# A decoder layer on one core: the places of matmul operands in memory, and a running product without an extra column

## The chip, the cores and the metric

The kernel runs on one core of a Trainium2 chip, in one launch. The core has TensorE (PE, the matmuls; its weight loads are listed apart as PEld), VectorE (DVE), ScalarE (ACT), GpSimd (POOL) and SyncE (SP), which here only issues transfers. Each has its own queue, in the order in which the program was written, and they meet at semaphores. The metric is device time in microseconds, the median of several runs. Lower is better.

## The reference

One decoder layer in float32: 1024 tokens of width 1024, and a final norm.

```python
h = rmsnorm(x, w_norm_mix)
proj = h @ w_mix_in                       # 1024 x 3592
y_sc = sc_b * causal_dwconv(sc_c * sc_h, w_sconv)
# gated delta rule in chunks of 64, 4 heads of 128, after a convolution and silu of q, k, v
y_gdn = rmsnorm(gated_delta_rule(q, k, v, g, beta), w_gdn_norm) * silu(z)
# stick-breaking attention, 4 heads of 64: for keys s < query t
#   A[t,s] = sigmoid(z_ts) * prod over s<j<t of (1 - sigmoid(z_tj));  y_sb = A @ v
x = x + concat([y_sc, y_gdn, y_sb]) @ w_mix_out
h = rmsnorm(x, w_norm_ffn)
gate, val = split(causal_dwconv(h @ w_ffn_up, w_ffn_conv))   # 2 x 2816 columns
x = x + (silu(gate) * val) @ w_ffn_down
return rmsnorm(x, w_norm_final)
```

## The kernel before

Every wide product is made of three fp32r matmuls: each operand is split into a rounded part h and a rest l, and h h, h l and l h are added up. A matmul has 128x128 weights and 512 moving columns. The program has four stages with such matmuls.

The input projection (lines 298 to 304, `mm_cm`) makes 26 column tiles of the projection. The moving operands are the activations xh and xl, four buffers each of the tag x8; the weights are tiles of the tags wh and wl, split from a loaded tile of the tag wr. The output projection (lines 1275 to 1296) has the output weights `wo` as moving operand (x8 again, after xh and xl are done) and the layer's outputs yh (tag s2) and yl (tag cv) as weights: 8 blocks of 48 matmuls, with transposes between. The up projection (line 1516, `product`) computes 22 pairs of column tiles with seven block products each, in the manner of Strassen; a product is 12 matmuls in a row. Its moving operands are the factors fB11, fB21, fB22, fT1 (tag e8) and fT2, fT3, fT4 (tag x8), and its weights come from `op_tile` (line 1449), which takes tiles of s2, wh, wl and wr in turn. The down projection (line 1682, `dn_mm`) has seven products of 11 slices, 12 matmuls each; `dn_tiles` (line 1640) takes both operands of a slice from the same list of tags, and its tiles' names end in the tag (P67wr, P67wh).

A tag is a set of equal buffers in SBUF, made by `T` (line 192) from one pool, in the order of their first use and with the size of the largest tile of the tag, rounded up to 32 bytes for each partition. In the built kernel, a tag's buffers so begin at these byte addresses modulo 256: x8 at 224; e8, cv and at at 32; wr, wh and wl, of 4224 bytes, at 32 and 160 in turn; the nine buffers of s2, of 2080 bytes (520 columns, line 204), each 32 further than the one before. A product's slices within a tile lie 512 or 2048 bytes apart.

From the input projection to the output projection the order of work on all engines is made by a planner, the class `Flow` (line 74): the parts of the layer are generators that yield requests (engine, estimated time, rank), wait for named events, and take and give counted buffers; the planner plays them against each other and records the instructions in the order in which it grants them. The wide matmuls of the projection are what PE gets between the pieces of attention, and then of the recurrence. From the up projection on, the order is written out by hand.

The attention works on pieces of 128 queries and up to 512 keys (`sb_piece`, line 606). ACT makes two sigmoids, om = 1 - sigmoid and sg = sigmoid; DVE runs a product from the last key to the first over om (line 641); POOL multiplies sg by om one column to the right (line 647), for which om has one more column: 1 for a query block's last piece (a memset, line 633) or else the carry out of the piece before (a copy, line 639). PE then transposes sg. In the recurrence, `prep2` (line 899) builds the inverse of a triangular block for every chunk of 128 tokens out of inverses of 32x32 blocks, in small matmuls (pw, py), after `inverse` (line 858) has run on DVE; `chain` (line 1095) then takes the chunks one after another.

Of the kernel before, what the change touches and what calls it, by code (L numbers as in the profile page):

```python
# [9 lines left out]
F32 = mybir.dt.float32  # L10
# [6 lines left out]
P = 128  # L17
# [4 lines left out]
GH = 4  # L22
# [162 lines left out]
def trunk(ctx: ExitStack, tc: tile.TileContext, xT, x, cst, wcm, wsv, wout, wnf, wup, wdn, wfin, out):  # L185
    nc = tc.nc
    sb = ctx.enter_context(tc.tile_pool(name="sb", bufs=1))
    dr = ctx.enter_context(tc.tile_pool(name="dr", bufs=1, space=DRAM))

    BUFS = dict(x8=8, e8=8, at=2, cv=4, s2=9, wr=2, wh=2, wl=2)  # L190

    def T(shape, dt, tag, name, bufs=None):
        return sb.tile(shape, dt, tag=tag, name=name, bufs=bufs or BUFS.get(tag, 1))

    def x8(shape, name, dt=F32):
        return T(shape, dt, "x8", name)

    def e8(shape, name, dt=F32):
        return T(shape, dt, "e8", name)
# [1 line left out]
    def cv(name, dt=F32, tag="cv"):  # L201
        return T([P, 1024], dt, tag, name)

    def s2(name, dt=F32, shape=(P, 520)):
        return T(list(shape), dt, "s2", name)

    def small(shape, name, bufs=1):
# [2 lines left out]
    def f32(ap):  # L210
        return ap.bitcast(F32)

    def copy(out_, in_, scale=None):
        if scale is None:
            nc.scalar.activation(out_, in_, AF.Copy)  # L215
        else:
            nc.scalar.activation(out_, in_, AF.Copy, scale=scale)  # L217

    def tt(eng, out_, a, b, op):
        eng.tensor_tensor(out_, a, b, op=op)  # L220
# [4 lines left out]
    mul, add, sub = ALU.mult, ALU.add, ALU.subtract  # L225
# [39 lines left out]
    def ms(name):  # L265
        return pp.tile([P, 512], F32, tag="ms", name=name, bufs=4)
# [53 lines left out]
    rb = T([P, L], F32, "rb", "rb")  # L320
# [17 lines left out]
    for ks in ((0,), (1,), (2, 3), (4, 5), (6, 7)):  # L338
        n = len(ks) * P
# [30 lines left out]
    fl = Flow(mm=2, ms=4, cv=1, s2=9, wr=2, wh=2, wl=2, at=2, e8=6, x8=0)  # L370

    def pe(ns, due=None):
        return "PE", ns, due, None

    def act(n, table=None, cls=None):
        return "ACT", T_ACT[0] + T_ACT[1] * n, cls, table

    def dve(n, port=True, per=T_DVE, cls=None):
        return "DVE", per[0] + per[1] * n, cls, port

    def pool(n, cls=None):
        return "POOL", T_POOL[0] + T_POOL[1] * n, cls, None

    def sp(kb, cls=None):
        return "SP", 2000 + 5 * kb, cls, None

    def take(tag, n=1):
        return "take", tag, n

    def wait(*what):  # L390
        return "wait", what

    def now(*what):
        fl.happen(what)
# [24 lines left out]
    def halves(r):  # L419
        return slice(64 * r, 64 * r + 64), slice(64 - 64 * r, 128 - 64 * r)  # L420
# [175 lines left out]
    for h in range(SH):  # L596
        for tb in range(NB):
            hi = (tb + 1) * P
            while hi > 0:
                lo = max(0, hi - 512)  # L600
                PIECES.append((h, tb, lo, hi))
                hi = lo
# [3 lines left out]
    def sb_piece(i, due):  # L606
        h, tb, lo, hi = PIECES[i]
        j, r = h // 2, h % 2
        own, _ = halves(r)
        n, w, nb = (tb + 1) * P, hi - lo, (hi - lo) // P  # L610
        nm = f"{h}_{tb}_{lo}"
        t = slice(tb * P, (tb + 1) * P)
        if i >= SB_AHEAD:
            yield wait("piece", i - SB_AHEAD)
        yield wait("sq", j, r)
        yield wait("sk", j, r)
        yield take("s2", 2)
        yield take("ms")
        yield pe(2 * max(60, w * 0.448) + (60 if hi == n else 0), due)
        pz = ms("pz" + nm)  # L620
        nc.tensor.matmul(pz[:, 0:w], lhsT=qa[j][:, r, t], rhs=kk_[j][:, r, lo:hi], start=True, stop=False)
        nc.tensor.matmul(pz[:, 0:w], lhsT=ql[j][:, r, t], rhs=kk_[j][:, r, lo:hi], start=False, stop=hi < n)
        if hi == n:
            nc.tensor.matmul(pz[:, w - P:w], lhsT=identr, rhs=causal, start=False, stop=True)
        yield act(w, "sig")
        sg, om = s2("sg" + nm), s2("om" + nm)
        nc.scalar.activation(om[:, 0:w], pz[:, 0:w], AF.Sigmoid, scale=-0.125)  # L627
        yield act(w, "sig")
        nc.scalar.activation(sg[:, 0:w], pz[:, 0:w], AF.Sigmoid, scale=0.125)
        fl.give("ms")  # L630
        if hi == n:
            yield pool(0)
            nc.gpsimd.memset(om[:, w:w + 1], 1.0)
            init = 1.0
        else:
            yield wait("scan", i - 1)
            yield pool(8)
            init = oms.pop(i - 1)[:, 0:1]
            nc.gpsimd.tensor_copy(om[:, w:w + 1], init)
        yield dve(w, per=T_SCAN)  # L640
        nc.vector.tensor_tensor_scan(om[:, 0:w][:, ::-1], om[:, 0:w][:, ::-1], om[:, 0:w][:, ::-1], init, op0=mul, op1=ALU.bypass)  # L641
        if hi < n:
            fl.give("s2")
        oms[i] = om
        now("scan", i)
        yield pool(w)
        tt(nc.gpsimd, sg[:, 0:w], sg[:, 0:w], om[:, 1:w + 1], mul)
        if lo == 0:
            fl.give("s2")
        yield take("ms")  # L650
        yield pe(109 * nb, due)
        pa = ms("pa" + nm)
        for b in range(nb):
            nc.tensor.transpose(out=pa[:, b * P:(b + 1) * P], in_=sg[:, b * P:(b + 1) * P], identity=ident)  # L654
        fl.give("s2")
        yield take("at")
        yield act(w)
        at = T([P, 4, 2, P], F32R, "at", "at" + nm)
        pav = pa[:, 0:w].rearrange("p (b t) -> p b t", b=nb)
        copy(at[:, 0:nb, 0, :], pav)  # L660
        yield dve(w, False)
        tt(nc.vector, at[:, 0:nb, 1, :], pav, f32(at[:, 0:nb, 0, :]), sub)
        fl.give("ms")
        if i > 0:
            yield wait("po", i - 1)
        for b in range(lo // P, hi // P):
            if i < 4:
                yield wait("v", b)
        if hi == n and tb % 2 == 0:
            yield take("ms")  # L670
            pos[h, tb // 2] = ms(f"po{h}_{tb}")
        po = pos[h, tb // 2]
        yield pe(118 * nb, due)
        for b in range(nb):
            s = lo // P + b
            nc.tensor.matmul(po[:, (tb % 2) * 256:(tb % 2) * 256 + 256], lhsT=vst[s // 4][:, s % 4, h * P:(h + 1) * P],
                             rhs=at[:, b, :, :].rearrange("p a t -> p (a t)"),
                             start=hi == n and b == 0, stop=lo == 0 and b == nb - 1)
        fl.give("at")
        now("po", i)  # L680
        now("piece", i)
        if i % PER == PER - 1:
            now("sb", j)
            fl.give("e8", 3 + 2 * j)
        if lo == 0 and tb % 2 == 1:
            pv = po.rearrange("p (a two t) -> p a two t", a=2, two=2)
            yield take("s2")
            yield act(256)
            yb = s2(f"yb{h}_{tb}")
            d = yb[:, 0:256].rearrange("p (a t) -> p a t", a=2)  # L690
            copy(d, pv[:, :, 1, :])
            yield dve(256, False)
            tt(nc.vector, d, pv[:, :, 0, :], d, add)
            fl.give("ms")
            yield dve(256)
            tt(nc.vector, yb[own, 256:512], yb[0:64, 0:256], yb[64:128, 0:256], add)
            yield sp(64)
            nc.sync.dma_start(yscr[6 + j, own, (tb - 1) * P:(tb + 1) * P], yb[own, 256:512])
            fl.give("s2")
            now("yb", h, tb)  # L700
# [9 lines left out]
    def gdn_gates():  # L710
# [45 lines left out]
        yield take("s2")  # L756
        yield pool(256)
        negtri = s2("negtri")[:, 0:P]
        nc.gpsimd.memset(negtri, -1.0)
        nc.gpsimd.affine_select(negtri, negtri, pattern=[[1, P]], compare_op=ALU.is_ge, fill=0.0, base=0, channel_multiplier=-1)  # L760
# [135 lines left out]
    H0, H1 = slice(0, 64), slice(64, 128)  # L896
    QB = [(slice(64 * p, 64 * p + 32), slice(64 * p + 32, 64 * p + 64)) for p in range(2)]

    def prep2(n):
# [13 lines left out]
        yield wait("TT", n // 2)  # L913
        Tt = st[n]["Tt"] = TT[n // 2][:, n % 2]
        yield pool(64)
        t64 = T([64, GH, 64], F32, "t64", f"t64{n}", bufs=2)
        nc.gpsimd.memset(t64, 0.0)
        for q in range(4):
            s = slice(32 * q, 32 * q + 32)
# [40 lines left out]
        pw2 = ms(f"pw2{n}")  # L960
        for h in range(GH):
            nc.tensor.matmul(pw2[H1, h * 64:(h + 1) * 64], lhsT=u[H0, h, H1], rhs=t64[:, h, :], start=True, stop=True)
        if n > 0:
            yield wait("py2", n - 1)
        yield act(256)
        w2 = T([P, GH, 64], F32, "w2", f"w2{n}")
        copy(w2[H1], pw2[H1, 0:256].rearrange("p (h c) -> p h c", h=GH))
        fl.give("ms")
        yield take("ms")
# [1 line left out]
        py2 = ms(f"py2{n}")  # L971
        for h in range(GH):
            nc.tensor.matmul(py2[H0, h * 64:(h + 1) * 64], lhsT=w2[H1, h, :], rhs=Tt[H1, h, H1], start=True, stop=True)
        now("py2", n)
        yield act(256)
        copy(Tt[H0, :, H1], py2[H0, 0:256].rearrange("p (h c) -> p h c", h=GH), scale=-1.0)
        fl.give("ms")
# [440 lines left out]
    for i in range(len(PIECES)):  # L1418
        first, per = DUE_SB[i // PER]
        fl.spawn(sb_piece(i, first + per * (i % PER)), 4)  # L1420
# [413 lines left out]
    for i in range(2, NF):  # L1834
        pr, n, more = Pair(i), i + 1, i + 1 < NF
# [161 lines left out]
```

## Times and profile before

| | |
|---|---|
| median of 3 runs | 1248.72 us (1248.26 to 1253.16) |
| the profiled execution | 1251.59 us |
| its span | 1249.8 us |
| instructions in the span | 16754 |
| mean granted clock of TensorE | 0.992 |

The span runs from the first instruction to the last one; the rest of the profiled execution's time lies around it. Starts are counted from the beginning of the span. [...] A group's busy time on PE is the time in which at least one matmul was under way.

### The profile page before, as it was taken

The page shows a single profiled execution, that of the slowest core. Times are in us where ns is not written, and L with a number is a line of the kernel's source. Part 1 is how long each engine was busy: PE and PEld are TensorE (multiplying, and loading weights), DVE is VectorE, ACT ScalarE, POOL GpSimd, SP SyncE. Part 2 cuts the span into 40 slices and gives each one's busy share as a digit, 9 for nine tenths or more (in the row PEclk, how much of TensorE's full clock was granted, in tenths as well). Part 3 has the DMA queues.
Part 4 walks back from the last instruction along what each step waited for, and adds up shares of the span by engine and source line. Part 5 has one row for each costly group of instructions (what it writes and reads, how often), then busy time and mean ns, then how long its engine had stood idle before and what let it go on. Part 6 is the DMA issues. An engine that isn't in the chain of part 4 may idle for free.

```text
span 1249.8 us, 16754 instructions
## 1 busy us (share of the span) xinstructions
PE 1213.9 (97%) x6131; PEld 997.8 (80%) x6131; DVE 930.5 (74%) x1317; ACT 640.1 (51%) x1088; POOL 406.4 (33%) x354
## 2 busy tenths in 40 slices
PE   7899999999999999999899999999999999999997
PEld 6798887888877887777688888888888877888886
DVE  3758889887964594445777888888888877965774
ACT  6757676986344543323554453554544534544454
POOL 2436443334243342014424444344342424001200
PEclk9999999999998999999999999999999999999999
DMA  9111233332434536434122333233331377952314
GB/s 340 56 52 37 67 116 120 116 92 75 131 108 114 134 98 197 136 117 152 34 68 93 126 110 101 72 98 125 108 111 60 110 268 257 330 180 77 106 51 147
DMA packets 87090, 152.76 MB, mean 122 GB/s; under 512 B 6592, under 2 KB 42464, under 8 KB 86752
## 3 DMA queue, kind: packets, MB, share of 16 engines
q1 hardware_dynamic: 86864, 151.59, 37.1%
q8 instruction: 48, 0.79, 0.3%
q14 instruction: 34, 0.28, 0.1%
q10 hardware_dynamic: 144, 0.10, 0.0%
HBM read 110.50 MB, written 41.17 MB: 121 GB/s over the span
## 4 chain that ended last, share of the span: by engine, by line
PE 52%; DVE 5%; DMA 3%; POOL 3%; ACT 3%; issue 2%; SPq 0%; POOLq 0%; ACTq 0%; DVEq 0%
PE pu L1516 16%; PE pdx L1682 8%; PE pz L1516 8%; PE pdzP L1682 7%; PE py L1516 4%; PE pmo L1292 1%; PE pmo L1296 1%; PE pmo L1294 1%; DMA m<-gscr 1%; DVE ua L223 1%; DVE h L223 1%; DVE xr L220 1%; ACT h L1309 1%; POOL ws L220 1%; DMA gaP<-gst 1%
## 5 line engine op out<-in xcount | busy, mean ns | idle before, releaser
L220 POOL TENSOR_TENSOR sg<-sg,om 128x512 f32<-128x512 f32 (+3 forms) x48 | 48.8, 1019 | 117.5 <-DVE om L641 93.8
L220 POOL TENSOR_TENSOR ws<-wu 128x512 f32<-128x512 f32 x43 | 66.7, 1569 | 44.5 <-DMA wu<-wup_in 36.6
L223 DVE SCALAR_TENSOR_TENSOR ua<-uv,ck,ua 128x1023 f32<-128x1023 f32 (+1 forms) x44 | 74.2, 1685 | 6.9 <-ACT ua L217 6.9
L223 DVE SCALAR_TENSOR_TENSOR ua<-ug,ck,ua 128x1023 f32<-128x1023 f32 (+1 forms) x44 | 75.2, 1709 | 0.7
L217 ACT ACTIVATE ua<-ug,ck 128x1024 f32<-128x1024 f32 x22 | 25.4, 1154 | 91.2 <-DVE ug L220 91.2
L1607 ACT ACTIVATE ua<-ua 128x1024 f32<-128x1024 f32 x22 | 23.3, 1060 | 68.6 <-DVE ua L223 68.6
L220 POOL TENSOR_TENSOR A<-wu,A 128x512 fp32r<-128x512 f32 x13 | 17.6, 1352 | 105.3 <-ACT A L215 98.3
L220 POOL TENSOR_TENSOR x<-x,wfb 128x512 f32<-128x512 f32 x8 | 12.8, 1635 | 117.8 <-ACT y L1698 117.8
L220 DVE TENSOR_TENSOR S<-ws,S 128x512 fp32r<-128x512 f32 x53 | 40.6, 770 | 11.9 <-ACT S L215 10.8
L1292 PE MATMUL pmo<-wo,yh 128*128 128x512 f32 x128 | 42.3, 412 | 2.8 <-ACT yh L215 1.9
L220 DVE TENSOR_TENSOR at<-pa,at 128x512 fp32r<-128x512 f32 (+3 forms) x48 | 26.4, 550 | 22.2 <-ACT at L215 22.1
L215 ACT ACTIVATE S<-ws 128x512 fp32r<-128x512 f32 x53 | 33.3, 629 | 18.4 <-PE py L1516 9.4
L220 POOL TENSOR_TENSOR h<-h,h 128x512 f32<-128x512 f32 x12 | 16.5, 1372 | 78.5 <-DVE h L223 70.7
L1294 PE MATMUL pmo<-wo,yh 128*128 128x512 f32 x128 | 40.7, 399 | 0.0
L1296 PE MATMUL pmo<-wo,yr 128*128 128x512 f32 x128 | 40.6, 399 | 0.0
L1516 PE MATMUL pz<-fT1h,S 128*128 128x512 f32 x112 | 37.5, 395 | 1.6 <-DVE S L220 1.1
L215 ACT ACTIVATE at<-pa 128x512 fp32r<-128x512 f32 (+3 forms) x48 | 23.2, 486 | 30.0 <-PE pa L654 28.3
L215 ACT ACTIVATE ug<-pu 128x512 f32<-128x512 f32 x44 | 26.2, 596 | 23.3 <-PE pu L1516 23.1
L220 DVE TENSOR_TENSOR ws<-ws,wu 128x512 f32<-128x512 f32 x22 | 27.0, 1227 | 14.6 <-POOL ws L220 14.6
L1516 PE MATMUL pu<-fT4h,A 128*128 128x512 f32 x104 | 35.9, 406 | 1.9 <-DVE uv L220 1.9
L220 DVE TENSOR_TENSOR A<-wu,A 128x512 fp32r<-128x512 f32 x24 | 25.2, 1052 | 14.2 <-ACT A L215 14.1
L641 DVE TENSOR_TENSOR_SCAN om<-om 128x512 f32<-128x512 f32 (+3 forms) x32 | 34.3, 1085 | 1.2 <-ACT om L627 1.1
(1456 smaller groups left out, 4040.2 us busy)
## 6 DMA issues: line engine op xcount, KB each, us to landing
wu<-wup_in SPq DMA_DIRECT2D x44, 512.0 KB, 3.8
gaP<-gst SPq DMA_DIRECT2D x77, 256.0 KB, 3.5
w<-wcm_in SPq DMA_DIRECT2D x23, 512.0 KB, 3.6
wd<-wdn_in SPq DMA_DIRECT2D x44, 256.0 KB, 5.0
gst<-g SPq DMA_DIRECT2D x12, 512.0 KB, 2.6
gst<-uv SPq DMA_DIRECT2D x10, 512.0 KB, 3.0
xs<-x_in SPq DMA_DIRECT2D x4, 1024.0 KB, 12.0
wor<-wout_in SPq DMA_DIRECT2D x8, 512.0 KB, 3.6
```

The lines of the kernel that those rows point to most:

```text
L215: nc.scalar.activation(out_, in_, AF.Copy)
L217: nc.scalar.activation(out_, in_, AF.Copy, scale=scale)
L220: eng.tensor_tensor(out_, a, b, op=op)
L223: nc.vector.scalar_tensor_tensor(out_, a, s, b, op0=op0, op1=op1)
L641: nc.vector.tensor_tensor_scan(om[:, 0:w][:, ::-1], om[:, 0:w][:, ::-1], om[:, 0:w][:, ::-1], init, op0=mul, op1=ALU.bypass)
L1292: nc.tensor.matmul(po[:, c * 512:(c + 1) * 512], lhsT=h, rhs=wh_[:, c * 512:(c + 1) * 512], start=first, stop=False)
L1294: nc.tensor.matmul(po[:, c * 512:(c + 1) * 512], lhsT=h, rhs=wl_[:, c * 512:(c + 1) * 512], start=False, stop=False)
L1296: nc.tensor.matmul(po[:, c * 512:(c + 1) * 512], lhsT=l, rhs=wh_[:, c * 512:(c + 1) * 512], start=False, stop=last)
L1309: nc.scalar.activation(h2, xr, AF.Square, accum_out=q2)
L1516: nc.tensor.matmul(o, lhsT=w[:, wk], rhs=b[:, k, :], start=first and k + j == 0, stop=k == 3 and j == 2, skip_group_check=not first)
L1607: nc.scalar.activation(self.acc, self.acc, AF.Silu)
L1682: nc.tensor.matmul(o, lhsT=a[:, tk], rhs=b, start=first and u == 0 and j == 0, stop=u == NU - 1 and j == 2, skip_group_check=not first)
```

## The change

There are four edits. First, the nine tags that hold large tiles get a pool of their own, with a size for each tag that is a multiple of 256 bytes (`BIG`; wr, wh and wl have 4352 bytes instead of 4224, s2 has 2048 instead of 2080), and a tile is a view of the first columns of a buffer; all other tiles move to a second pool, `sm`, behind it. In the built kernel all buffers of these nine tags begin at 128 modulo 256. Second, s2 loses its eight additional columns, so the attention can't keep the carry there: the memset and the copy go, the product over sg runs on columns 0 to w - 2, and in a piece with a carry a second product of one column multiplies the last column of sg by it, after the scan instead of before. Third, w2 has no tile of its own but takes the lower half of the tile whose upper half is t64, of which there are two, and a wait between successive chunks goes. Fourth, the scratch that the program keeps for descriptors of transfers shrinks to 1024 bytes.

```diff
--- before.py
+++ after.py
@@ -185,12 +185,24 @@
 def trunk(ctx: ExitStack, tc: tile.TileContext, xT, x, cst, wcm, wsv, wout, wnf, wup, wdn, wfin, out):
     nc = tc.nc
     sb = ctx.enter_context(tc.tile_pool(name="sb", bufs=1))
+    sm = ctx.enter_context(tc.tile_pool(name="sm", bufs=1))
     dr = ctx.enter_context(tc.tile_pool(name="dr", bufs=1, space=DRAM))
 
-    BUFS = dict(x8=8, e8=8, at=2, cv=4, s2=9, wr=2, wh=2, wl=2)
+
+    BIG = dict(x8=(8, 8192), e8=(8, 8192), at=(2, 4096), cv=(4, 4096), s2=(9, 2048), wr=(2, 4352), wh=(2, 4352), wl=(2, 4352), rb=(1, 4096))
 
     def T(shape, dt, tag, name, bufs=None):
-        return sb.tile(shape, dt, tag=tag, name=name, bufs=bufs or BUFS.get(tag, 1))
+        if tag not in BIG:
+            return sm.tile(shape, dt, tag=tag, name=name, bufs=bufs or 1)
+        n, size = BIG[tag]
+        cols = 1
+        for c in shape[1:]:
+            cols *= c
+        t = sb.tile([P, size // 4], dt, tag=tag, name=name, bufs=n)[:, 0:cols]
+        if len(shape) == 2:
+            return t
+        ax = " ".join("abc"[:len(shape) - 1])
+        return t.rearrange(f"p ({ax}) -> p {ax}", **dict(zip("abc", shape[1:])))
 
     def x8(shape, name, dt=F32):
         return T(shape, dt, "x8", name)
@@ -201,7 +213,7 @@
     def cv(name, dt=F32, tag="cv"):
         return T([P, 1024], dt, tag, name)
 
-    def s2(name, dt=F32, shape=(P, 520)):
+    def s2(name, dt=F32, shape=(P, 512)):
         return T(list(shape), dt, "s2", name)
 
     def small(shape, name, bufs=1):
@@ -628,23 +640,20 @@
         yield act(w, "sig")
         nc.scalar.activation(sg[:, 0:w], pz[:, 0:w], AF.Sigmoid, scale=0.125)
         fl.give("ms")
-        if hi == n:
-            yield pool(0)
-            nc.gpsimd.memset(om[:, w:w + 1], 1.0)
-            init = 1.0
-        else:
+        init = 1.0
+        if hi < n:
             yield wait("scan", i - 1)
-            yield pool(8)
             init = oms.pop(i - 1)[:, 0:1]
-            nc.gpsimd.tensor_copy(om[:, w:w + 1], init)
         yield dve(w, per=T_SCAN)
         nc.vector.tensor_tensor_scan(om[:, 0:w][:, ::-1], om[:, 0:w][:, ::-1], om[:, 0:w][:, ::-1], init, op0=mul, op1=ALU.bypass)
-        if hi < n:
-            fl.give("s2")
         oms[i] = om
         now("scan", i)
+        if hi < n:
+            yield pool(8)
+            tt(nc.gpsimd, sg[:, w - 1:w], sg[:, w - 1:w], init, mul)
+            fl.give("s2")
         yield pool(w)
-        tt(nc.gpsimd, sg[:, 0:w], sg[:, 0:w], om[:, 1:w + 1], mul)
+        tt(nc.gpsimd, sg[:, 0:w - 1], sg[:, 0:w - 1], om[:, 1:w], mul)
         if lo == 0:
             fl.give("s2")
         yield take("ms")
@@ -913,7 +922,8 @@
         yield wait("TT", n // 2)
         Tt = st[n]["Tt"] = TT[n // 2][:, n % 2]
         yield pool(64)
-        t64 = T([64, GH, 64], F32, "t64", f"t64{n}", bufs=2)
+        t64 = T([P, GH, 64], F32, "t64", f"t64{n}", bufs=2)
+        w2, t64 = t64, t64[H0]
         nc.gpsimd.memset(t64, 0.0)
         for q in range(4):
             s = slice(32 * q, 32 * q + 32)
@@ -960,10 +970,7 @@
         pw2 = ms(f"pw2{n}")
         for h in range(GH):
             nc.tensor.matmul(pw2[H1, h * 64:(h + 1) * 64], lhsT=u[H0, h, H1], rhs=t64[:, h, :], start=True, stop=True)
-        if n > 0:
-            yield wait("py2", n - 1)
         yield act(256)
-        w2 = T([P, GH, 64], F32, "w2", f"w2{n}")
         copy(w2[H1], pw2[H1, 0:256].rearrange("p (h c) -> p h c", h=GH))
         fl.give("ms")
         yield take("ms")
@@ -971,7 +978,6 @@
         py2 = ms(f"py2{n}")
         for h in range(GH):
             nc.tensor.matmul(py2[H0, h * 64:(h + 1) * 64], lhsT=w2[H1, h, :], rhs=Tt[H1, h, H1], start=True, stop=True)
-        now("py2", n)
         yield act(256)
         copy(Tt[H0, :, H1], py2[H0, 0:256].rearrange("p (h c) -> p h c", h=GH), scale=-1.0)
         fl.give("ms")
@@ -1987,7 +1993,7 @@
         wsv=con(sv.reshape(KT, P, 264).transpose(1, 0, 2)),
         wout=con(f(w_mix_out)[0]), wnf=con(f(w_norm_ffn)), wup=pack(f(w_ffn_up)[0], up_cols),
         wdn=con(f(w_ffn_down)[0]), wfin=con(f(w_norm_final)[None, :]))
-    nc = bacc.Bacc("TRN2", target_bir_lowering=False, num_devices=1)
+    nc = bacc.Bacc("TRN2", target_bir_lowering=False, num_devices=1, dynamic_dma_scratch_size=1024)
     aps = {n: nc.dram_tensor(n + "_in", a.shape, F32, kind="ExternalInput").ap() for n, a in arrays.items()}
     out = nc.dram_tensor("out_dram", (L, D), F32, kind="ExternalOutput").ap()
     with tile.TileContext(nc) as tc:
```

Because the planner sees other requests, its order changes up to the output projection. On GpSimd, in the first head of the attention (sg and om numbered by head, query block and first key; w3l to w5l are rests of projection weights), before:

```order
L220 TENSOR_TENSOR sg0_3_0_549<-sg0_3_0_549,om0_3_0_550 128x512
L220 TENSOR_TENSOR w3l_715<-w3_388,w3h_698 128x1024
L633 MEMSET om0_4_128_713 128x1
L633 MEMSET om0_5_256_743 128x1
L220 TENSOR_TENSOR sg0_4_128_712<-sg0_4_128_712,om0_4_128_713 128x512
L639 COPY om0_4_0_739<-om0_4_128_713 128x1
L220 TENSOR_TENSOR sg0_5_256_742<-sg0_5_256_742,om0_5_256_743 128x512
L639 COPY om0_5_0_776<-om0_5_256_743 128x1
L220 TENSOR_TENSOR sg0_4_0_738<-sg0_4_0_738,om0_4_0_739 128x128
L220 TENSOR_TENSOR w4l_807<-w4_419,w4h_761 128x1024
```

and now:

```order
L232 TENSOR_TENSOR sg0_3_0_551<-sg0_3_0_551,om0_3_0_552 128x511
L232 TENSOR_TENSOR sg0_4_128_636<-sg0_4_128_636,om0_4_128_637 128x511
L232 TENSOR_TENSOR sg0_4_0_689<-sg0_4_0_689,om0_4_128_637 128x1
L232 TENSOR_TENSOR sg0_4_0_689<-sg0_4_0_689,om0_4_0_690 128x127
L232 TENSOR_TENSOR w3l_733<-w3_391,w3h_717 128x1024
L232 TENSOR_TENSOR sg0_5_256_705<-sg0_5_256_705,om0_5_256_706 128x511
L232 TENSOR_TENSOR w4l_797<-w4_422,w4h_783 128x1024
L232 TENSOR_TENSOR sg0_5_0_780<-sg0_5_0_780,om0_5_256_706 128x1
```

The memsets and copies are gone, the products of one column stand ahead of the product of the same tile, and the pieces 4 and 5 stand ahead of the split of w3 and w4 instead of around them.

On PE, where the input projection ends (pd24 and pd25 are its last tiles) and the output projection begins (pmo0 is its first block; pyt, pv, pk, p and pco belong to the recurrence, numbered by chunk), before:

```order
L304 MATMUL pd24_4284<-xh3_104,w24l_3578 128x512 x2
L1185 MATMUL pyt6_4674<-ident_67,on6_4661 128x128 x4
L1185 MATMUL pyt7_4681<-ident_67,on7_4672 128x128 x4
L300 MATMUL pd25_4285<-xh3_104,w25h_4250 128x512 x2
L302 MATMUL pd25_4285<-xl3_105,w25h_4250 128x512 x2
L304 MATMUL pd25_4285<-xh3_104,w25l_4254 128x512 x2
L1292 MATMUL pmo0_4705<-wo2_4515,yh00_4518 128x512 x2
L1294 MATMUL pmo0_4705<-wo2_4515,yh00_4518 128x512 x2
```

and now:

```order
L316 MATMUL pd25_3791<-xh3_107,w25l_3751 128x512 x2
L1093 MATMUL pv6_4466<-ident_70,ld6_4007 128x128 x4
L1093 MATMUL pv7_4477<-ident_70,ld7_4201 128x128 x4
L1036 MATMUL pk6_4482<-ident_70,ld6_4007 128x128 x4
L1036 MATMUL pk7_4487<-ident_70,ld7_4201 128x128 x4
L1298 MATMUL pmo0_4495<-wo2_4138,yh00_4122 128x512 x2
L1300 MATMUL pmo0_4495<-wo2_4138,yh00_4122 128x512 x2
L1302 MATMUL pmo0_4495<-wo2_4138,yr0_4121 128x512 x2
```

Before, the recurrence was over when the output projection began; now its chunks 5 to 7 are still to come, and stand between the groups of pmo0. Further on in the same block, now:

```order
L1163 MATMUL pco6_4655<-S6_4447,ld6_4007 128x128
L1164 MATMUL pco6_4655<-vn6_4602,m26_4415 128x128
L1124 MATMUL p27_4672<-r7_4664,Tt6_4065 128x128 x4
L1298 MATMUL pmo0_4495<-wo0_3942,yh00_4122 128x512 x2
L1300 MATMUL pmo0_4495<-wo0_3942,yh00_4122 128x512 x2
L1302 MATMUL pmo0_4495<-wo0_3942,yr0_4121 128x512 x2
```

The block's part wo0, which needs the outputs y of the short convolution, comes after 36 wide matmuls of the block, as before, but now 72 narrow matmuls of the recurrence stand among these. The first matmul of `prep2` (pw) comes after 1148 wide matmuls; before it came after 1112.

## Rows read from the trace of the kernel before

**Rows 1.** The page, part 1: busy us, share of the span, instructions of each engine.

```profile
PE 1213.9 (97%) x6131; PEld 997.8 (80%) x6131; DVE 930.5 (74%) x1317; ACT 640.1 (51%) x1088; POOL 406.4 (33%) x354
```

**Rows 2.** Busy time by stretch: length; busy us (instructions) by engine, clock, DMA share, GB/s.

```profile
355.00:495.00 140.00, 131.51 (x1132) 113.13 (x1132) 85.03 (x183) 62.22 (x149) 56.57 (x70) 0.98 0.42 120
640.00:960.00 320.00, 320.00 (x1384) 260.04 (x1383) 272.42 (x263) 150.39 (x232) 125.77 (x80) 1.00 0.30 99
```

**Rows 3.** Chain that ended last, down projection: start us, us, what.

```profile
1061.21 30.18 PE pdzP L1682 x132
```

**Rows 4.** Timeline of PE, down projection: start us, us, line, out<-in, sizes, count.

```profile
1107.72 2.89 PE L1682 MATMUL pdx<-P66wh,P66wl 128*128 128x512 f32 x12
1110.45 2.95 PE L1682 MATMUL pdx<-P67wr,P67wh 128*128 128x512 f32 x12
1113.24 2.93 PE L1682 MATMUL pdx<-P68wl,P68wr 128*128 128x512 f32 x12
1116.01 2.88 PE L1682 MATMUL pdx<-P69cv 128*128 128x512 f32 x12
1118.73 2.44 PE L1682 MATMUL pdx<-P 128*128 128x512 f32 x10
```

**Rows 5.** Timeline of PE, up projection: first matmul of three successive products.

```profile
831.90 0.40 PE L1516 MATMUL pu<-fB11h,A 128*128 128x512 f32 x1
...
834.70 0.39 PE L1516 MATMUL pz<-fT1h,S 128*128 128x512 f32 x1
...
837.42 0.40 PE L1516 MATMUL pu<-fT4h,A_11h 128*128 128x512 f32 x1
```

**Rows 6.** Timeline of PE, input projection: tile w20, first and last piece of w21.

```profile
338.19 0.62 PE L300 MATMUL pd<-xh,w20h 128*128 128x512 f32 x2
...
339.57 0.63 PE L300 MATMUL pd<-xh,w21h 128*128 128x512 f32 x2
...
343.30 0.63 PE L304 MATMUL pd<-xh,w21l 128*128 128x512 f32 x2
```

**Rows 7.** Timeline of PE, output projection: first and last row of one stretch.

```profile
520.75 0.63 PE L1294 MATMUL pmo<-wo,yh 128*128 128x512 f32 x2
...
525.41 0.62 PE L1296 MATMUL pmo<-wo,yr 128*128 128x512 f32 x2
```

**Rows 8.** Waits of PE: us in total, times, longest us.

```profile
PE pu L1516 <- DVE uv L220: 2.0, 2, 1.9
PE pk L1030 <- ACT w L215: 2.0, 1, 2.0
PE pmo L1292 <- ACT yh L215: 1.9, 1, 1.9
...
PE pmo L1292 <- DVE a_sch L220: 0.9, 1, 0.9
```

**Rows 9.** Chain that ended last, before the output projection.

```profile
484.08 1.23 DVE a_sch L220
...
485.32 5.53 DMA yscr<-a_sch
...
490.87 3.74 DMA yr<-yscr
```

**Rows 10.** Busy time by stretch, three short stretches of a lower clock.

```profile
392.80:399.70 6.90, 6.71 (x32) 5.64 (x31) 3.92 (x10) 1.88 (x7) 1.07 (x5) 0.51 0.00 0
495.30:498.70 3.40, 3.40 (x9) 2.64 (x9) 1.50 (x3) 1.15 (x2) 0.00 (x0) 0.51 0.45 165
625.00:628.40 3.40, 3.40 (x10) 2.64 (x9) 3.18 (x5) 2.54 (x3) 0.00 (x0) 0.50 0.02 5
```

**Rows 11.** Groups of GpSimd, the attention: count, busy us, mean ns, idle before.

```profile
L220 POOL TENSOR_TENSOR sg<-sg,om 128x512 f32<-128x512 f32 x24 | 30.5, 1272 | 67.0 <-DVE om L641 61.2 <-ACT sg L629 1.9 <-DVE yb L220 1.6
...
L639 POOL COPY om<-om 128x1 f32<-128x1 f32 x16 | 6.1, 381 | 0.0
...
L633 POOL MEMSET om<- 128x1 f32 x32 | 2.8, 100 | 0.0
```


## The prediction

> **What bounds the kernel now.** I read the page's first part, then busy time by stretch, then the order of work on PE, and the waits last. PE is busy 97% of the span, but its matmuls overlap [rows 1], so a full PE shows little; what counts is the spacing of successive starts. From 640 to 960 us PE runs without a pause, 1384 matmuls in 320 us, 231.2 ns each, and DVE, the next engine, is busy 272 of the 320 [rows 2]. The chain that ended last is one unbroken piece of PE in the down projection, 132 matmuls in 30.18 us, 228.6 ns each [rows 3]. So in the up and down projections the time is the number of matmuls times their spacing, and nothing else is late.
>
> That spacing isn't constant. All these matmuls have 128x128 weights and 512 columns, yet a group of twelve takes, by the distance between starts, 2.73 us (P66), 2.79 (P67), 2.77 (P68) and 2.72 (P69) [rows 4]. Beside this I put the places of the tiles in the built kernel, the byte address in a partition modulo 256. P66 has both operands at 160; P67 has the moving one at 160 and the weights at 32, 128 apart; P68 and P69 have both at 32. In the up projection, the product with fB11 (at 32; its weights at 160) takes 2.80 us, and the next one, fT1 with weights both at 32, takes 2.72 [rows 5]. In the input projection the moving tiles lie at 224: w20 (at 160, 192 apart) runs at 1.38 us for six, 230 ns, and w21 (at 32, 64 apart) at 3.73 us for sixteen, 233 ns [rows 6]. So matmuls are slower where the moving rows and the weights loaded meanwhile (those of the next matmul) start at different places modulo 256. It also has a memory: P68 is aligned but follows P67, and takes 2.77 where P69, one group later, takes 2.72 [rows 4]. Settled, a matmul takes 2.72 us / 12 = 226.8 ns; one group after a disturbance, 230.8.
>
> [...]
>
> **The change part by part, against the profiled execution's own 1251.6 us (span 1249.8 and 1.8 around it).**
>
> *The tiles' places.* All operands of the wide matmuls now lie at 128 modulo 256 in the built kernel, so every pair is aligned. Up projection, 22 pairs x 84 = 1848 matmuls: 231.2 to 226.8 ns, 4.4 ns each, 8.1 us. DVE covers it: 272 us of work against 320 x 226.8/231.2 = 314. Down, 7 x 11 x 12 = 924: 228.6 to 226.8, 1.7 us; most pairs are aligned already. Output projection, 8 x 48 = 384: 20 matmuls take 4.66 us, 233.0 each [rows 7]; transposes break it into stretches of 12 to 24, so I take the middle of 230.8 and 226.8, 228.8: 1.6 us. Input projection, 26 x 48 = 1248: mean of 230 and 233.1, 231.6; most of it stands in runs of 6 or 12 between attention pieces, the rest in runs of 96 and more, so 229.5: 2.6 us. Sum 14.0 us. Bounds: 0 if the places aren't the cause; 18.2 if all four stages settle at 226.8 at once (8.1 + 1.7 + 2.4 + 6.0). I take 14.0, being nearest to the rows. The 264-column matmuls keep rows of 1056 bytes, so nothing changes for them; for the narrow fp32 ones, whose aligned price no row shows, I take nothing.
>
> *The carry.* 32 memsets (2.8 us) and 16 copies of 381 ns (6.1 us) leave GpSimd, 8.9 us in all, and 16 products of one column come, at the price of the copies at most [rows 11]. The big product shrinks by one column. GpSimd is busy 33% [rows 1] and mostly waits for the scan there (61.2 us) [rows 11], so by itself this is 0; were GpSimd the bound there, it would give 2.8 us. A carried piece no longer waits for a memset or a copy in the written order, so attention pieces go to PE earlier.
>
> *The order up to the output projection.* The planner's result is new there. The inverse's matmuls (pw) now follow 36 more wide matmuls than before, and the last chunks of the recurrence lie inside the first output block instead of before it. Before, that block stops for data: the wait of 1.9 us for yh and of 0.9 us for a_sch [rows 8] end a chain of 1.23 + 5.53 + 3.74 = 10.5 us (multiply, store, load) [rows 9], against which PE has 36 wide matmuls, 8.4 us. [...] Now 72 narrow matmuls of the recurrence stand beside the 36 wide ones, so the wait and the half clock should go: 4.5 us. What is late next is the recurrence itself, each hop PE, DVE or ACT, PE, with six wide matmuls (1.4 us) between; I give back 1 us and count 3.5. Bounds: +6 (three more waits of 2.0 us as for pk [rows 8]) and -8 (the four waits of rows 8 together, 6.8 us, and most of one half clock's 1.7).
>
> *The rest.* w2 shares a buffer with t64 (two instead of one), which removes a wait among eight short steps; the smaller DMA scratch concerns a queue that the page doesn't list. Both 0.
>
> Sum: 1251.6 - 14.0 - 3.5 = 1234.1 us. The median of the runs is 1248.72, 2.9 under the profiled execution, so the forecast is 1231 us.
>
> **Rivals.**
> 1. *The rhythm doesn't settle.* After P67 twelve aligned matmuls were not enough [rows 4]; if DVE and ACT writes or the short runs keep disturbing it, aligned matmuls stay halfway, about 229.0 everywhere but in the down projection: 4.1 + 0 + 1.5 + 3.2 = 8.8, with the 3.5 of the front 1248.7 - 12.3 = 1236; with nothing from the front 1240. For: P68. Against: fT1 lies 41 KB from its weights and settles within its own twelve [rows 5].
> 2. *The places are not the cause.* The 2.79 belongs to something that goes with those buffers. Then only the front moves: 1245, between 1241 and 1255. Against: it holds in three stages with different tiles. [...]
> 3. *Slower: the recurrence's tail is bare.* It starts 36 x 233 ns = 8.4 us later, and eight chunks must pass with six wide matmuls per hop. If each chunk waits 2.0 us as pk does once now, and each wait draws a half clock of 3.4 us, 1.7 lost, that is 8 x 3.7 = 29.6 us; less 14.0, 1264. It decides from the fourth chunk on: 4 x 3.7 = 14.8 eats the alignment. For: PE is busy 131.5 of 140 us there, its worst stretch [rows 2]. Against: longest wait 2.0, once.
> 4. *More in the front.* All its waits go: 1248.7 - 14.0 - 8 = 1227, and with settled 18.2, 1222.
>
> **How the numbers follow.** Forecast 0.68, rival 1 0.15, rival 2 0.07, rival 3 0.03, rival 4 0.07. The forecast's own range is 1225 to 1237; to hold 8 in 10 I go from 1222 (rival 4) to 1241 (rival 1 without the front). A measurement tells 0.5%, 6.2 us, from no change, so faster means under 1242.5: the forecast, rivals 1 and 4 and a little of 2, 0.91; same is most of rival 2 and a mild rival 3, 0.06; slower 0.03.
>
> **What would show it.** In the profile after, 640 to 950 us should hold a matmul every 226 to 228 ns, in every product alike, and the chain of 132 in the down projection should last about 29.9 us; with 231 and 30.2 rival 2 is right, with 229 rival 1. The output projection should begin without the wait for yh and without the half clock behind it. I am wrong if the up projection gains under 3 us, or if waits of PE between 355 and 500 us grow by more than 10.

## The result, and the profile after

The changed kernel takes 1230.89 us (median of 6 runs, 1228.66 to 1235.40) against 1249.65 (6 runs, 1248.26 to 1253.16): a ratio of 0.9854, interval 0.983 to 0.9877, 18.8 us less. Its profiled execution took 1234.68 us (span 1232.9), near the upper end of its runs. The engines' busy times, from the page's first part [rows 1]:

```profile
PE 1197.8 (97%) x6131; PEld 996.1 (81%) x6131; DVE 938.1 (76%) x1317; ACT 635.1 (52%) x1085; POOL 411.8 (33%) x322
```

The shares are nearly those of before and say nothing of the 17 us between the two profiled executions. Busy time by stretch does, in the columns of [rows 2]:

```profile
355.00:495.00 140.00, 135.45 (x1156) 117.27 (x1155) 98.03 (x182) 63.21 (x151) 58.20 (x73) 0.98 0.43 124
640.00:960.00 320.00, 320.00 (x1413) 264.97 (x1412) 280.42 (x266) 148.07 (x231) 135.19 (x86) 1.00 0.33 107
...
495.30:498.70 3.40, 3.40 (x19) 2.74 (x17) 2.17 (x4) 3.04 (x6) 0.00 (x0) 1.00 0.58 174
...
1014.00:1017.40 3.40, 3.40 (x9) 2.64 (x9) 3.30 (x4) 0.03 (x1) 0.00 (x0) 0.52 1.04 379
```

Between 640 and 960 us PE starts 1413 matmuls instead of 1384, one every 226.5 ns instead of 231.2. At 495 us, where the granted clock was 0.51 [rows 10], it is 1.00. But at 1014 us there is a half clock, 0.52, that before did not have: nine matmuls in 3.40 us, where at 1.00 seventeen stand, as in a second trace of the changed kernel:

```profile
1014.00:1017.40 3.40, 3.40 (x17) 2.82 (x16) 3.22 (x6) 3.40 (x6) 0.00 (x0) 1.00 1.06 395
```

The timeline of PE, with a row from each place that was read before (start us, us, line, out<-in, sizes, count; in brackets the wait ahead of the row and what ended it). A group of twelve is listed with 2.88 us while the next one starts 2.72 us after it, so rates are read from the starts:

```profile
329.00 0.62 PE L312 MATMUL pd<-xh,w20h 128*128 128x512 f32 x2
...
339.88 0.62 PE L312 MATMUL pd<-xh,w21h 128*128 128x512 f32 x2
...
503.88 0.62 PE L1298 MATMUL pmo<-wo,yh 128*128 128x512 f32 x2
...
508.43 0.62 PE L1300 MATMUL pmo<-wo,yh 128*128 128x512 f32 x2
...
818.42 0.39 PE L1522 MATMUL pu<-fB11h,A 128*128 128x512 f32 x1
...
821.14 0.39 PE L1522 MATMUL pz<-fT1h,S 128*128 128x512 f32 x1
...
823.86 0.39 PE L1522 MATMUL pu<-fT4h,A_11h 128*128 128x512 f32 x1
...
1008.82 2.91 PE L1688 MATMUL pdx<-P10wh,P10wl 128*128 128x512 f32 x12
1013.77 0.49 PE L1522 MATMUL pu<-fT4h,A_21h 128*128 128x512 f32 x1 [2.04 <-DVE uv L232]
...
1092.11 2.88 PE L1688 MATMUL pdx<-P66wh,P66wl 128*128 128x512 f32 x12
1094.83 2.88 PE L1688 MATMUL pdx<-P67wr,P67wh 128*128 128x512 f32 x12
1097.55 2.88 PE L1688 MATMUL pdx<-P68wl,P68wr 128*128 128x512 f32 x12
1100.27 2.88 PE L1688 MATMUL pdx<-P69cv 128*128 128x512 f32 x12
```

Tile w20's 48 matmuls take 10.88 us, 226.7 ns each, where it was 230 [rows 6]; 20 of the output projection take 4.55 us instead of 4.66 [rows 7]; the products with fB11 and fT1 take 2.72 us both, instead of 2.80 and 2.72 [rows 5]; and P66, P67 and P68 start 2.72 us apart, so the group that cost 2.79 is gone [rows 4]. The chain that ended last holds the same 132 matmuls of the down projection, in 29.92 us instead of 30.18 [rows 3]:

```profile
1046.03 29.92 PE pdzP L1688 x132
```

The waits of PE (us in total, times, longest):

```profile
PE pu L1522 <- DVE uv L232: 2.8, 2, 2.0
PE p L1140 <- ACT vn L227: 2.3, 1, 2.3
PE pa L663 <- POOL sg L232: 2.1, 3, 1.3
...
PE pk L1036 <- ACT t L227: 1.3, 1, 1.3
```

The output projection's two waits, 1.9 us for yh and 0.9 for a_sch [rows 8], are gone. In their place stands one of 2.3 us in the recurrence, and GpSimd's sg is waited for with 2.1 us. On GpSimd the groups of the attention's product, by form (columns as in [rows 11]):

```profile
L232 POOL TENSOR_TENSOR sg<-sg,om 128x511 f32<-128x511 f32 x24 | 31.7, 1322 | 47.3 <-DVE om L648 29.8 <-ACT sg L641 5.9 <-issue 4.7
...
L232 POOL TENSOR_TENSOR sg<-sg,om 128x1 f32<-128x1 f32 x16 | 5.8, 361 | 21.9 <-ACT sg L641 21.0 <-POOL sg L232 0.9
```

A product of one column costs 361 ns where the copy cost 381, and the memsets' 2.8 us are gone. But a product of 511 columns takes 1322 ns where one of 512 took 1272, and GpSimd's busy time as a whole rose from 406.4 to 411.8 us, so as a whole nothing was freed there.

### The profile page after: what moved, and what is told of

Its sections match the earlier page's. It is cut to its first block, busy times and chain, and to the rows that moved or that the text cites. A ratio compares the mean times of both kernels' runs of the same rounds, so it can differ in the third digit from the quotient of the medians.

```text
span 1232.9 us, 16696 instructions
## 1 busy us (share of the span) xinstructions
PE 1197.8 (97%) x6131; PEld 996.1 (81%) x6131; DVE 938.1 (76%) x1317; ACT 635.1 (52%) x1085; POOL 411.8 (33%) x322
## 4 chain that ended last, share of the span: by engine, by line
PE 78%; DVE 7%; ACT 6%; DMA 5%; issue 3%; POOL 1%; SPq 1%; POOLq 0%; ACTq 0%; DVEq 0%
PE pu L1522 18%; PE pz L1522 9%; PE pdx L1688 8%; PE pdzP L1688 7%; PE pd L312 5%; PE pd L314 5%; PE pd L316 5%; PE py L1522 4%; PE pmo L1302 2%; PE pmo L1300 2%; PE pmo L1298 2%; DMA m<-gscr 2%; PE po L685 1%; DMA xs<-x_in 1%; PE pa L663 1%
## 5 line engine op out<-in xcount | busy, mean ns | idle before, releaser
L232 POOL TENSOR_TENSOR sg<-sg,om 128x511 f32<-128x511 f32 (+3 forms) x64 | 60.6, 957 | 118.0 <-DVE om L648 62.1
L1522 PE MATMUL pu<-fT2h,S 128*128 128x512 f32 x104 | 34.2, 389 | 0.0
```

Source lines behind the costliest of these rows:

```text
L1522: nc.tensor.matmul(o, lhsT=w[:, wk], rhs=b[:, k, :], start=first and k + j == 0, stop=k == 3 and j == 2, skip_group_check=not first)
```

## The experiments

I had two theories for the places (the distance between a matmul's moving rows and weights, modulo 256 bytes, sets its spacing; or it is something else in those buffers), and two for the rest (the new order is worth about 3.5 us; or it is worth more, and the places less).

**Places alone.** The order of all instructions is that of before, carry and w2 too; only the places differ, and the scratch for descriptors, which is 1024 bytes in this kernel and in the next as in the changed one. A tile of s2 keeps its 520 columns, in buffers of 2304 bytes.

```diff
--- before
+++ places alone
+    sm = ctx.enter_context(tc.tile_pool(name="sm", bufs=1))
...
-    BUFS = dict(x8=8, e8=8, at=2, cv=4, s2=9, wr=2, wh=2, wl=2)
+    BIG = dict(x8=(8, 8192), e8=(8, 8192), at=(2, 4096), cv=(4, 4096), s2=(9, 2304), wr=(2, 4352), wh=(2, 4352), wl=(2, 4352), rb=(1, 4096))
```

> The kernel before in its own order on every engine, with the carry column kept, but with the large tiles at 128 modulo 256 bytes (s2 buffers of 2304 bytes). Theory (places of the operand pairs set the spacing of matmuls): the spacing falls from 231 to about 227 ns in the up projection and from 228.6 to 226.8 in the down projection, 14 us in all, so about 1235 to 1236 us. Rival (the places are not the cause, the planner's new order is): 1249 us. Second rival (the rhythm alone does a part): 1240.

1238.19 us (1236.06 to 1240.3) against 1249.69, ratio 0.9905 (0.9884 to 0.9925): 11.5 us less by the medians, and 9.4 to 14.5 by the interval. Busy time by stretch:

```profile
640.00:960.00 320.00, 320.00 (x1414) 265.01 (x1413) 280.42 (x269) 151.94 (x237) 130.70 (x84) 1.00 0.33 104
...
493.60:497.00 3.40, 3.40 (x9) 2.63 (x8) 1.29 (x2) 1.15 (x2) 0.00 (x0) 0.50 0.44 149
```

The up projection has the changed kernel's rate, and the half clock at the output projection's beginning is still there.

**Order alone.** The changed kernel's carry, w2 and order, with the places of before modulo 256. (In the built kernels the carry alone gives this order row by row; the edit to w2 alone gives that of before.)

```diff
--- before
+++ order alone
+        init = 1.0
+        if hi < n:
...
+            tt(nc.gpsimd, sg[:, w - 1:w], sg[:, w - 1:w], init, mul)
+            fl.give("s2")
...
+        tt(nc.gpsimd, sg[:, 0:w - 1], sg[:, 0:w - 1], om[:, 1:w], mul)
```

> The changed kernel's order, carry and shared w2 buffer, instruction for instruction, but with the tiles at their old places (8 of 9 s2 buffers, and wr, wh, wl, at other places modulo 256 than the moving operands). Theory: only the front moves, by the 3.5 us of the waits before the output projection, so 1245 to 1246 us, and the up projection keeps 231 ns. Rival (the order is the cause): 1231 us.

1243.13 us (1241.74 to 1244.46), ratio 0.9945 (0.9926 to 0.9965): 6.6 us less by the medians (4.4 to 9.2 by the interval), some 2 to 3 us more than expected.

```profile
640.00:960.00 320.00, 320.00 (x1385) 259.92 (x1384) 274.12 (x262) 148.24 (x229) 127.03 (x81) 1.00 0.31 101
...
495.30:498.70 3.40, 3.40 (x19) 2.80 (x18) 2.61 (x4) 2.62 (x4) 0.00 (x0) 1.00 0.59 181
```

The mirror image: the old rate, and the half clock gone. By the medians the two parts are 11.5 + 6.6 = 18.1 us, against 18.8 for the whole change; by the ratios they are 18.7 against 18.2. Within the noise they add up. The smaller scratch is in both parts, so a gain of its own would be counted twice in these sums; they leave no room for one beyond the noise.

**The distance as a dose.** In the changed kernel wr, wh, wl and s2, the up projection's weights, move by 64, 128 or 192 bytes against the moving tiles (48 of its 1848 matmuls take weights of another tag and stay at 0); the order stays.

```diff
--- after
+++ 64 bytes further (128: 32 columns, 192: 48)
+    sw = ctx.enter_context(tc.tile_pool(name="sw", bufs=1))
+    sw.tile([P, 16], F32, tag="pad", name="pad", bufs=1)
...
-        t = sb.tile([P, size // 4], dt, tag=tag, name=name, bufs=n)[:, 0:cols]
+        t = (sw if tag in ("wr", "wh", "wl", "s2") else sb).tile([P, size // 4], dt, tag=tag, name=name, bufs=n)[:, 0:cols]
```

> The changed kernel with one empty tile of 64 bytes ahead of the tags wr, wh, wl and s2, the weights of the wide matmuls: in the input, output and up projections weights and moving operands lie 64 bytes apart, all with one another as before. Theory (distance of the pair modulo 256): 233 ns in the up projection, as rows of the kernel before had at that distance, 6.3 x 1848 = 11.6 us, and 4 us in the other two, so about 1247 us; the down projection, whose pairs lie in one tag or in two shifted ones, stays at 226.8. Rival (any layout whose buffers are multiples of 256 bytes is as good, what counted was the odd size of the buffers): 1231 us.

> The changed kernel with wr, wh, wl and s2 128 bytes further than the other large tiles. If the price rises from 192 over 128 to 64 bytes (228.9 and 233.3 ns in the up projection at the ends, 2.79 us for twelve at 128 in the kernel before, 232.5 each): 231 to 232.5 ns, about 1241 to 1244 us. If 128 is a special case at one side or the other: 229 ns and 1237 us, or 233.3 and over 1245.

> The same with an empty tile of 192 bytes: weights 192 bytes above the moving operands modulo 256. Theory by rows of the kernel before at that distance (230 ns): 3.3 x 1848 = 6.1 us in the up projection and 1 us in the others, about 1238 us, between the changed kernel and the shift of 64. Rival (any misaligned distance costs the same): as the shift of 64.

64: 1244.53 us, ratio 0.9957 (0.9941 to 0.9974). 128: 1240.33, a single run. 192: 1237.63, ratio 0.9898 (0.9869 to 0.9928). The stretch from 640 to 960 us, 64 first:

```profile
640.00:960.00 320.00, 320.00 (x1373) 257.85 (x1372) 271.76 (x261) 149.43 (x230) 125.91 (x80) 1.00 0.32 101
```

128:

```profile
640.00:960.00 320.00, 320.00 (x1378) 259.46 (x1377) 273.08 (x261) 147.41 (x226) 127.93 (x83) 1.00 0.32 101
```

192:

```profile
640.00:960.00 320.00, 320.00 (x1400) 262.56 (x1399) 277.33 (x263) 148.58 (x229) 136.43 (x86) 1.00 0.33 106
```

That is 233.1, 232.2 and 228.6 ns a matmul, against 226.5 at distance 0. Over all pairs of successive 512-column starts in the up projection, pauses left out, it is 233.3, 232.4 and 228.9 against 226.8. So with the order of all instructions unchanged the rate follows the distance. The times of 64 and 128 came out a little lower than the rates let me expect.

**One tag alone,** wr 64 bytes further, to see the memory again.

```diff
-        t = (sw if tag in ("wr", "wh", "wl", "s2") else sb).tile([P, size // 4], dt, tag=tag, name=name, bufs=n)[:, 0:cols]
+        t = (sw if tag in ("wr",) else sb).tile([P, size // 4], dt, tag=tag, name=name, bufs=n)[:, 0:cols]
```

> The changed kernel with only the tag wr 64 bytes further on modulo 256, for one look at the spacing. In the down projection only the slices with a wr operand (wr,wh and wl,wr, two of seven in succession) are misaligned. Theory with a memory: these two take 2.79 to 2.80 us for twelve matmuls, the next slice (cv, both tiles aligned) still 2.76 to 2.77, and the one after that 2.72. Rival without a memory: the cv slice takes 2.72 at once.

1234.52 us, a single run. PE in the down projection:

```profile
1090.91 2.88 PE L1690 MATMUL pdx<-P66wh,P66wl 128*128 128x512 f32 x12
1093.63 2.93 PE L1690 MATMUL pdx<-P67wr,P67wh 128*128 128x512 f32 x12
1096.40 2.96 PE L1690 MATMUL pdx<-P68wl,P68wr 128*128 128x512 f32 x12
1099.19 2.91 PE L1690 MATMUL pdx<-P69cv 128*128 128x512 f32 x12
1101.94 2.88 PE L1690 MATMUL pdx<-P 128*128 128x512 f32 x12
```

2.72, 2.77, 2.79, then 2.75 for P69, which is aligned, and 2.72 again (the next group starts at 1104.66): the slow groups are those with wr, and the one behind them still pays part.

These rows also bear on a rival that I had not named: that moved tiles slow PE by the writes of DVE and ACT into them, and not by what PE reads. While P67 runs, DVE writes only tiles of wh and wl, which have not moved, and for as long as beside every other group; ACT writes the same two.

```profile
1094.49 0.69 DVE L234 TENSOR_TENSOR P32wh<-wd,P32wh 128x512 fp32r<-128x512 f32 x1 [1.43 <-ACT P32wh L229]
1095.10 0.68 DVE L234 TENSOR_TENSOR P32wl<-gaP,P32wl 128x512 fp32r<-128x512 f32 x1
```

**The input projection alone.** The weights of its last 23 tiles (of 26) lie 64 bytes into their buffers; all else is aligned.

```diff
--- after
+++ input projection 64 bytes off
+            return T([P, 1040], dt, tag, name)[:, 16:1040]
```

> The changed kernel with the weights of the input projection's last 23 tiles 64 bytes further on in their buffers, all else in place: 1104 matmuls go back from 229.5 to about 233 ns, 3.8 us of PE's time, in the front alone. Theory that the front gives the alignment's gain back in waits for the recurrence and its half clocks: the time rises by at most 1.5 us, to 1231 to 1232.5. Rival (PE's spacing counts there in full, as in the prediction): 1235.

1234.08 us (1233.07 to 1236.08), ratio 0.988 (0.9862 to 0.9899). The spacing over the whole input projection is 232.4 ns instead of 229.5, and the time 3.2 us above the changed kernel's first median, 2.0 above its later one (1232.08, below); the ranges overlap. Against what I expected, more than half of the spacing's 2.8 ns x 1248 = 3.5 us shows in the time.

**The wait at 1013.77.** In the changed kernel DVE splits four operands of the down projection ahead of the sum uv for which PE waits, as its timeline shows:

```profile
1010.62 0.69 DVE L232 TENSOR_TENSOR P11wr<-wd,P11wr 128x512 fp32r<-128x512 f32 x1
...
1012.42 0.69 DVE L232 TENSOR_TENSOR P12wr<-gaP,P12wr 128x512 fp32r<-128x512 f32 x1
1013.03 0.69 DVE L232 TENSOR_TENSOR uv<-pu,uv 128x512 f32<-128x512 f32 x1
```

I put the sum first.

```diff
--- after
+++ uv first
+    prev.e7()
     dn_op("P1", 1)
     dn_op("P1", 2)
     dn_part(0)
-    prev.e7()
```

> The changed kernel with one statement moved: the addition to uv of the last pair (prev.e7) is written ahead of the operands of the down projection's slices 1 and 2 instead of behind them, so DVE has 2.4 us less ahead of it. Theory (the up projection's gain is cut at its end by this wait of 2.0 us and the half clock behind it, 1.7 us): up to 3.7 us less, 1227 to 1229. Rival (the wait moves to the operands of slice 1): 1231.

1233.99 us (1233.12 to 1235.4), ratio 0.9876 (0.9858 to 0.9893): no gain. The wait and its half clock are gone, and another pair stands some 15 us later, for an operand of the down projection that is now late (between them PE also waits 1.5 us for another operand, P13cv, with no half clock behind it). Busy time by stretch, and that row of PE's timeline:

```profile
1014.00:1017.40 3.40, 3.40 (x17) 2.71 (x15) 2.31 (x3) 1.60 (x3) 0.00 (x0) 1.00 1.05 386
1029.60:1033.00 3.40, 3.40 (x10) 2.62 (x9) 3.40 (x6) 0.00 (x0) 3.40 (x1) 0.50 0.68 197
```

```profile
1028.44 4.74 PE L1688 MATMUL pdx<-P15cv 128*128 128x512 f32 x11 [2.52 <-DVE P15cv L232]
```

**The narrow operands.** Identity, masks and ones at 128 modulo 256, and the 264-column weights in rows of 1280 bytes.

```diff
--- after
+++ narrow ones aligned
-    ck = small([P, C_N], "ck")
+    ck = small([P, 256], "ck")[:, 0:C_N]
...
+            return T([P, 4, 320], dt, tag, name)[:, :, 0:264]
```

> The changed kernel with the remaining operands aligned too: identity, causal mask, ones and t64 at 128 modulo 256 (they are at 192), and the 264-column weights in rows of 1280 bytes instead of 1056. Theory (the distance matters for these as well): about 192 x 5 ns for the 264-column matmuls and up to 384 x 2 ns for the transposes, 1 to 2 us, so 1229 to 1230, some of it given back in the front. Rival (narrow matmuls are bound by their weight loads): 1231.

1232.19 us (1229.5 to 1233.25), ratio 0.9857 (0.9838 to 0.9876): the changed kernel's time. The zero that I had put for them stands, as far as a spread of some 4 us shows it.

**Another common place.** All large tiles at 0 instead of 128 modulo 256: first in a single run, then in five beside five of the changed kernel itself.

```diff
--- after
+++ base 0
+    sb.tile([P, 32], F32, tag="pad", name="pad", bufs=1)
```

> The changed kernel with all its large tiles 128 bytes further, so that they begin at 0 instead of 128 modulo 256; their distances from each other and the order of work stay. If only the distance of a matmul's two operands counts: 226.8 ns a matmul in the up projection as in the changed kernel, about 1231 us. If the place itself counts: another spacing, 228 ns or more, 1235 us or more.

> The kernel with all large tiles at 0 modulo 256 again, now timed, beside the changed kernel itself. Its one look gave 1226.2 us, 2.4 under the fastest run of the changed kernel. If only the distance between operands counts, that look was one with few stretches of half clock: the median here is that of the changed kernel within 3 us, 1229 to 1233, ratio 0.985 to 0.987. If 0 is a better place than 128: 1226 to 1228, ratio 0.982 or less.

> The changed kernel unchanged, on the same chip and in the same rounds as the one with the tiles at 0 modulo 256. 1229 to 1233 us, ratio 0.985 to 0.987 by either theory.

The single run took 1226.2 us. In the five, base 0 has 1229.01 (1227.88 to 1230.95), ratio 0.9833 (0.9808 to 0.9857), and the changed kernel 1232.08 (1230.37 to 1233.4), ratio 0.9855 (0.9828 to 0.9883). The single run's stretch, the stretch around a wait of its timeline, and the row of that wait:

```profile
640.00:960.00 320.00, 320.00 (x1413) 264.99 (x1412) 280.24 (x266) 150.90 (x235) 134.20 (x85) 1.00 0.33 105
...
1006.00:1009.40 3.40, 3.10 (x13) 2.55 (x14) 3.40 (x5) 0.44 (x1) 0.00 (x0) 1.00 1.03 380
```

```profile
1006.30 0.50 PE L1523 MATMUL pu<-fT4h,A_21h 128*128 128x512 f32 x1 [1.88 <-DVE uv L233]
```

The rate is that of the changed kernel, 1413 in 320 us: with the distances unchanged, the common places 0 and 128 give the same. Half clocks explain a part of the 3 us. The changed kernel timed again has one at 408 us that both traces of base 0 lack:

```profile
408.00:411.40 3.40, 3.40 (x13) 2.83 (x12) 3.40 (x5) 0.00 (x0) 3.12 (x6) 0.50 1.11 301
```

That is 1.7 of the 2.5 us by which the spans of the two timed traces differ. Over the five runs of each, though, the mean granted clock is 0.9954 and 0.9948, which is 0.7 us; the rest stays open, and so does whether base 0 draws fewer half clocks by its places or by chance. It is the fastest version measured, by 0.2 to 0.25%, with ranges that still overlap.

## Why the prediction was right, and where two terms of it were not

The forecast was 1231 us and the time is 1230.89, with a mechanism that the experiments bear out. But two misses cancel, so that it is right to 0.1 us is luck. *The tiles' places* were put at 14.0 us and give 11.5 or 12.2 (to the kernel before, or to the order alone); *the order* was put at 3.5 and gives 6.6 or 7.3. The times alone rule out 3.5 (the interval is 4.4 to 9.2), but not 14.0 (9.4 to 14.5); that miss rests on the traces. To see which part of each was off, I divided the traces at the first matmul of the up projection and at its last, and summed the 3.4 us stretches of half clock, found by going through the spans in short stretches. A stretch at half clock does about half its work (in 3.40 us nine wide matmuls at 0.52, seventeen at 1.00), so I count it with half its length.

| us | start of up | half clock before | up, length | half clock in it | up's end to down's end |
|---|---|---|---|---|---|
| before | 587.6 | 13.6 | 444.3 | 3.4 | 210.3 |
| places alone | 584.4 | 10.2 | 435.8 | 3.4 | 208.7 |
| order alone | 579.9 | 6.8 | 444.8 | 3.4 | 210.4 |
| after | 579.8 | 10.2 | 438.2 | 6.8 | 207.2 |
| after, again | 576.7 | 3.4 | 435.8 | 3.4 | 208.4 |

*Up and down projection: right.* Without the half clocks the places take 8.4 us off the up projection alone, and 8.3 to 9.0 with the new order; the prediction said 8.1, from 4.4 ns by 1848, and the spacing fell by 4.6 (231.4 to 226.8). DVE covered it, with 280 of 320 us. The down projection gave 1.7 to 3.2; predicted 1.7.

*Input and output projection: the spacing right, its worth too large.* The spacing fell from 231.8 to 229.5 ns and from 232.5 to 228.3, within 0.5 ns of 229.5 and 228.8. That is 2.9 + 1.6 = 4.5 us of matmuls, predicted 4.2; yet the up projection starts only 3.2 us earlier by the places alone, of which 1.7 is half clock: 1.5. With the new order it is 1.8 (0.1 and 1.7) or, in the second trace, 1.5 (3.2 less 1.7). So 1.5 to 1.8 of 4.2 arrives. This term was mis-sized: it counted matmuls by spacing where PE also stops for pieces of attention and recurrence that don't get faster. One such stop can be seen. After 1100 matmuls of the input projection the places alone are 1.9 us ahead (375.5 us instead of 377.4), of 2.5 by spacing. Then PE waits in the recurrence as follows, before and with the places alone:

```profile
PE py L947 <- ACT w L215: 0.7, 1, 0.7
```

```profile
PE py L958 <- ACT w L226: 2.0, 1, 2.0
```

That takes back 1.3 us. It is one pair of traces; that such waits take all of the rest is argued, not shown. And the loss is not fixed: base 0, with the same spacing, starts the up projection at 572.6 and 573.8 us with no half clock ahead of it, so by the same account, against the order alone, 3.9 and 2.7 us arrive. Also, the experiment on the input projection alone speaks against a full loss, with 2.3 to 2.6 of its 3.5 us at the up projection's start by the same account (578.95 us, 3.4 at half clock).

*The order: mechanism right, size off.* In one pair of traces the up projection starts 7.7 us earlier by the order alone. The two waits of the output projection are 2.8 of it. (Of the 72 narrow matmuls counted beside its first 36 wide ones, 56 stand among them and 16 just ahead of them.) The half clock behind them was counted with 1.7, half of the 3.40 us at 0.51 in [rows 10], so that both made 4.5; but 6.8 us at half clock less stand in the table, because the stretch of 6.8 us at 392.8 [rows 10] has become one of 3.4 at 409: 3.4 us. (Nor is that fixed: the changed kernel's first trace has two there, at 396 and 410, its second one, at 408.) And the 1 us that I gave back for the recurrence didn't have to be paid: another 1.5 was won, which I can lay to no single wait. 2.8 + 3.4 + 1.5 is 7.7.

*The carry and the rest:* nothing by themselves, as said. What the carry did is the order.

*The rivals.* That the rhythm doesn't settle is refuted by the 29.92 us and by P67; that the places are not the cause, by the places alone and by the dose. The recurrence's bare tail came true in one chunk: the wait of 2.3 us for vn, with a half clock behind it at 410 us. More in the front was half right: the order gave 6.6 to 7.3 us of the 8 that it put there, but the places did not give 14.0 beside it.

*What was late next* I had not named: the crossing from up to down. PE waits 2.04 us there for uv, 0.68 in the order alone. Taking this wait away moved it to P15.

## What to carry to other kernels

Where wide matmuls follow each other without a pause, read their spacing by groups of equal shape; if it differs, compare the groups' addresses, and lay the operands at one place modulo 256 bytes: here it took 1 to 2% off such matmuls (231.8 to 229.5 ns in the input projection, 231.4 to 226.8 in the up projection). Count that in full only where PE waits for nothing else; where it does, between a third and nine tenths arrived in the traces here. And an edit to another engine's small instructions can be worth more by what a planner makes of it than by its own time.

## What the runs showed of the hardware

The price by the distance of the weights from the moving rows, modulo 256 bytes, in the up projection: 0 bytes 226.8 ns (the changed kernel), 64 bytes 233.3, 128 bytes 232.4, 192 bytes 228.9 (the three shifts).

The length of the wait ahead of it did not settle the half clock here. In the changed kernel 1.08 us for S had 3.4 us at 0.51 behind it; with base 0 (the single run) the same wait of 1.08 us had none, and neither had one of 2.15 us for uv. The waits and the stretches behind them, the changed kernel first:

```profile
601.27 1.22 PE L1522 MATMUL pz<-fT1h,S 128*128 128x512 f32 x2 [1.08 <-DVE S L232]
```

```profile
601.20:604.60 3.40, 3.33 (x8) 2.65 (x9) 3.40 (x5) 2.15 (x4) 1.67 (x1) 0.51 0.08 18
```

```profile
594.14 0.73 PE L1523 MATMUL pz<-fT1h,S 128*128 128x512 f32 x2 [1.08 <-DVE S L233]
...
609.73 0.50 PE L1523 MATMUL pu<-fT4h,A 128*128 128x512 f32 x1 [2.15 <-DVE uv L233]
```

```profile
594.00:597.40 3.40, 3.26 (x14) 2.73 (x15) 3.40 (x5) 2.07 (x4) 1.68 (x1) 1.00 0.21 22
610.00:613.40 3.40, 3.40 (x16) 2.79 (x16) 3.27 (x5) 2.44 (x3) 0.00 (x0) 1.00 0.02 5
```

Part of the spread between runs follows from that: over the runs on record, the granted clock accounts for about half of the variance of a kernel's span (correlation 0.7). In three traces it accounts for nearly all: up to the end of the down projection base 0 had no half clock and a span of 1224.5 us, timed again one (3.4 us) and 1226.2, the changed kernel 17.0 us and 1232.9; what follows the down projection takes 7.7 or 7.8 us in all three. Half of 17.0 on 1224.5 is 1233.0, half of 3.4 is 1226.2.
